# Linear attention of a decoder step: TensorE issues in the written order from the first head's gates on, small products gathered, output products one main product behind the state's

## The chip, the cores and the metric

The kernel runs on one core of one Trainium2 chip. Its time is the device time of one execution in microseconds (us), from the first to the last instruction and what lies around them. The five engines are named as in the profile: PE (TensorE matmuls; PEld are its weight loads), DVE (VectorE), ACT (ScalarE), POOL (GpSimd) and SP (SyncE, which issues most DMAs). Each engine works through its own queue in a fixed order, and semaphores make it wait for the others.

## The reference

One inference step of a two-layer decoder, for 512 new prompt positions and 8 decode positions, width 1024. Layer 0 mixes by windowed attention, layer 1 by gated linear attention (GLA); each is followed by a gated convolutional FFN, and each of the four parts ends in a LayerNorm. The change lies in the GLA, of which the reference computes, for each of 4 heads and in chunks of 64 positions:

```python
b = jnp.cumsum(lc, axis=2)                  # lc: log decay, from a product of rank 16
q_in = qc * jnp.exp(b)
k_in = kc * jnp.exp(-b)
att = jnp.where(causal, jnp.einsum('bhtd,bhsd->bhts', q_in, k_in), 0.0)
o = jnp.einsum('bhts,bhsv->bhtv', att, vc) + jnp.einsum('bhtd,bhdv->bhtv', q_in, S)
S_new = jnp.exp(b_last[:, :, 0, :, None]) * S + jnp.einsum('bhsd,bhsv->bhdv', kc * jnp.exp(b_last - b), vc)
...
o = o * lax.rsqrt(jnp.mean(jnp.square(o), -1, keepdims=True) + NORM_EPS) * norm_g
o = (o * jax.nn.silu(g)).reshape(B, T, GLA_DV)
return o @ w_o, s_new
```

## The kernel before

All activations lie transposed (channels on partitions). The positions are cut into two groups: `a`, the first 256 prompt positions, and `b`, the other 256 with the 8 decode positions. The weights come in units of 128 output channels. `plan` lists the units: for the GLA a rank-16 product for the decay (`gla_rank`), and per head one unit for q, one for k, two for v and two for the gate g; then 8 units of the output projection. `order` lets group b follow group a at a distance of 4 or 5 units. One unit of one group is a *main product*: `product` issues 24 matmuls (8 contraction blocks, times three terms of a high and low split in fp32r; L173 to L175) into one of 4 accumulator banks `accp`. The FFN's are the same or in a wider form (L191, L192).

Between main products lie the *small products* in plain fp32: the decay's (L681), the masked scores of a head (`att`, L730), the transposes of k and v (L750 to L752), the state's update `up` (L767), the two terms of the output `o` (L775 from the old state, L778 from the scores), the transposes of the normalised output for the gate (L866, L868), and those of the decode positions (L814 to L816, L827, L828). They use four more PSUM banks: `tp` (one), `pv` (one), `sc` (two).

The code is written as generators: `yield n` lets n main products pass ("slots") before the rest of a step is emitted; `due` resumes what has come due behind each main product. That sets the order in which the program is *written*. A list scheduler then orders each engine's queue by its own estimate of times, so the queue of PE may differ from the written order, and small products can come to stand inside a main product. `manual_schedule` over an engine keeps the written order on that engine. The weights of unit u+6 are loaded (SP, L156), rounded (ACT, L158) and reduced to their low part `wl` (DVE, L161) while unit u runs.

`ln_end` ends a LayerNorm: sums on PE (L256), the reciprocal root `r` on ACT and DVE (L267 to L277), subtraction of the mean on POOL and DVE (L263), then per channel block a product with r (`u`, L296), scaling on ACT (L297, the high part `xh` or `xs`) and POOL (L298), and the low part on DVE (L301, `xl` or `xs`). The main products of the next part wait for these.

Of the kernel before, what the change touches and what calls it, by code (L numbers as in the profile page):

```python
# [11 lines left out]
F32 = mybir.dt.float32  # L12
F32R = mybir.dt.float32r
I32 = mybir.dt.int32
AF = mybir.ActivationFunctionType
# [5 lines left out]
P = 128  # L21
# [70 lines left out]
class Net:  # L92
# [624 lines left out]
    def gla_k(self, g, u, h):  # L717
        nc, n = self.nc, g.n
        ps = self.product(g, u, g.xh, g.xl)
        yield 1  # L720
        g.k = self.gp.tile([P, n], F32, name=f"k_{g.name}")
        nc.vector.tensor_tensor(g.k, ps, g.em, op=ALU.mult)
        if g.i:
            g.kraw = self.gp.tile([P, NS], F32, name="kraw", bufs=2)
            nc.vector.tensor_copy(g.kraw, ps[:, 256:])
        yield 1
        att = self.mtile("sc")
        for b in range(2):
            bs = slice(b * P, (b + 1) * P)
            nc.tensor.matmul(att[:, bs], g.k[:, bs], g.q[:, bs], start=True, stop=True)  # L730
        g.att = self.attm[self.attm_i % 2]
        self.attm_i += 1
        nc.vector.copy_predicated(g.att, self.causal.unsqueeze(1).broadcast_to([P, 2, P]), att[:, :256].rearrange("p (b t) -> p b t", b=2))

    def gla_v(self, g, u, h, i):
        nc, n = self.nc, g.n
        ps = self.product(g, u, g.xh, g.xl)
        vt = self.gp.tile([P, n], F32, name=f"v{i}_{g.name}")
        nc.scalar.copy(vt, ps)
        if i == 0:  # L740
            g.v0 = vt
            return
        yield 1
        q, k, v0, v1, att, eb = g.q, g.k, g.v0, vt, g.att, g.eb
        ctx = dict(q=q, k=k, v0=v0, v1=v1, ep=g.ep, kraw=g.kraw) if g.i else None
        vks = []
        for b in range(2):
            bs = slice(b * P, (b + 1) * P)
            mp = self.mtile("tp")
            nc.tensor.transpose(mp[:, 0:P], k[:, bs], self.ident)  # L750
            nc.tensor.transpose(mp[:, P:2 * P], v0[:, bs], self.ident)
            nc.tensor.transpose(mp[:, 2 * P:3 * P], v1[:, bs], self.ident)  # L752
            vk = self.gp.tile([P, 3 * P], F32, name="vk", bufs=2)
            nc.scalar.copy(vk, mp[:, :3 * P])
            vks.append(vk)
        if g.i:
            self.spawn(self.gla_sample(g, h, **ctx), 0)
        yield 1
        o = self.mtile("pv")
        small = self.gp.tile([P, 8], F32, name="gsmall", bufs=2)  # L760
        st = self.tst[:, h]
        for b in range(2):
            bs = slice(b * P, (b + 1) * P)
            ob = o[:, b * 256:(b + 1) * 256]
            first = g.i == 0 and b == 0
            up = self.mtile("sc")[:, :256]
            nc.tensor.matmul(up, vks[b][:, 0:P], vks[b][:, P:], start=True, stop=True)  # L767
            if first:
                nc.vector.tensor_copy(st, up)
            else:  # L770
                f = self.gp.tile([P, 1], F32, name="f", bufs=2)
                nc.vector.tensor_tensor(f, self.ebl[:, h:h + 1], eb[:, 2 * b:2 * b + 1], op=ALU.mult)
                sp = self.gp.tile([P, 256], F32, name="sp", bufs=2)
                nc.vector.tensor_scalar(sp, st, f, None, op0=ALU.mult)
                nc.tensor.matmul(ob, q[:, bs], sp, start=True, stop=False)  # L775
                nc.vector.tensor_tensor(st, up, sp, op=ALU.add)
            nc.vector.tensor_copy(self.ebl[:, h:h + 1], eb[:, 2 * b + 1:2 * b + 2])
            nc.tensor.matmul(ob, att[:, b], vks[b][:, P:], start=first, stop=True)  # L778
        if g.i:
            so = self.gp.tile([P, 256], F32, name="sp", bufs=2)  # L780
            nc.vector.tensor_scalar(so, st, self.ebl[:, h:h + 1], None, op0=ALU.mult)
            nc.scalar.dma_start(out=self.O["gla_p"][h], in_=so)
        on = self.gp.tile([P, 512], F32, name="on", bufs=2)
        for b in range(2):
            ob = o[:, b * 256:(b + 1) * 256]
            nc.scalar.activation(on[:, b * 256:(b + 1) * 256], ob, AF.Square, accum_out=small[:, b:b + 1])
        rs = self.rms(small[:, 0:8], P, 2)
        for b in range(2):
            bs = slice(b * 256, (b + 1) * 256)
            nc.scalar.activation(on[:, bs], o[:, bs], AF.Copy, scale=rs[:, b:b + 1])  # L790
        g.on = on
# [13 lines left out]
    def gla_sample(self, g, h, q, k, v0, v1, ep, kraw):  # L805


        nc, st, g.st = self.nc, g.st, []
        nc.vector.tensor_copy(self.qz.rearrange("p (t x) -> p t x", t=2)[:, :, 0:P:32],
                              q[:, 256:].rearrange("p (t j) -> p t j", t=2))  # L810
        pr = self.gp.tile([P, NS], F32, name="qk")
        nc.vector.tensor_tensor(pr, q[:, 256:], k[:, 256:], op=ALU.mult)
        mp = self.mtile("tp")
        nc.tensor.transpose(mp[:NS, 0:P], v0[:, 256:], self.ident)  # L814
        nc.tensor.transpose(mp[:NS, P:2 * P], v1[:, 256:], self.ident)
        nc.tensor.matmul(mp[:NS, 256:257], pr, self.eps[:, 1:2], start=True, stop=True)  # L816
        vs = self.vs
        nc.vector.tensor_copy(vs[:NS], mp[:NS, :257])
        dv = self.dram.tile([NS, 256], F32, name="dv")
        nc.sync.dma_start(out=dv, in_=vs[:NS, :256])  # L820
        nc.vector.tensor_scalar(self.qkd[:NS].rearrange("p (j s) -> p s j", j=4)[:, 0:2],
                                self.ident[:NS, :NS].rearrange("p (t j) -> p t j", t=2), vs[:NS, 256:257], None, op0=ALU.mult)
        yield 1
        os_ = self.mtile("sc")[:, :256]
        for b in range(NS):
            r = slice(32 * (b % 4), 32 * (b % 4) + 32)
            nc.tensor.matmul(os_[r], self.qz[:, 32 * b:32 * b + 32], st[b // 2][:, b % 2], start=b < 4, stop=False)  # L827
        nc.tensor.matmul(os_, self.qkd, vs[:, :256], start=False, stop=True)  # L828
        small = self.gp.tile([P, 4], F32, name="ssmall")
        jk = self.gp.tile([P, 256], F32, name="sp", bufs=2)  # L830
        nc.scalar.activation(jk, os_, AF.Square, accum_out=small[:, 0:1])
        rs = self.rms(small, P, 1)
        g.os = self.gp.tile([P, 256], F32, name="osamp")
        nc.scalar.activation(g.os, os_, AF.Copy, scale=rs)
        yield SPAUSE if h < GH - 1 else SPAUSEL
        late = self.tc.keep_in_program_order
        for p in range(4):
            s = st[p]
            vb = self.gp.tile([P, 2, 256], F32, name="vb")
            nc.sync.dma_start(out=vb, in_=dv[2 * p:2 * p + 2].unsqueeze(0).broadcast_to([P, 2, 256]))  # L840
            yield 1
            for j in range(2):
                b = 2 * p + j
                late(nc.scalar.activation(s[:, j], s[:, j], AF.Copy, scale=ep[:, 256 + b:257 + b]))
                late(nc.vector.scalar_tensor_tensor(s[:, j], vb[:, j], kraw[:, b:b + 1], s[:, j], op0=ALU.mult, op1=ALU.add))  # L845
            nc.sync.dma_start(out=self.O["gla_s"][2 * p:2 * p + 2, h].rearrange("b k v -> k b v"), in_=s)
            if h < GH - 1:
                g.st.append(self.state_load(h + 1, p))
        if h == GH - 1:
            self.close(self.gp_cm)  # L850

    def gla_g(self, g, u, h, i):
        nc, n = self.nc, g.n
# [6 lines left out]
        nc.vector.reciprocal(e, e)  # L860
        sg = self.gp.tile([P, NT - 256], F32, name="sg", bufs=3)[:, :n]
        nc.vector.tensor_tensor(sg, ps, e, op=ALU.mult)
        yield 3 - i
        tp = self.mtile("tp")
        for b in range(2):
            nc.tensor.transpose(tp[:, b * P:(b + 1) * P], g.on[:, b * 256 + i * P:b * 256 + (i + 1) * P], self.ident)  # L866
        if g.i:
# [92 lines left out]
    def run(self):  # L960
        nc = self.nc
        self.plan()
        self.nu, self.extra, self.close_wx = WSLOTS, {}, False
        self.attn_open()
        self.later, self.slot, self.seq, self.pool_mark = [], 0, 0, None
        for i, u in self.order():
            g = self.groups[i]
            _, _, f, a, pre = self.units[u]
            if i == 0 and pre:
# [134 lines left out]
```

## Time and profile before

| | |
|---|---|
| median of 3 runs | 1148.62 us (1147.16 to 1149.75) |
| the profiled execution | 1146.73 us, of which the span of the instructions is 1144.7 us |
| mean granted clock of PE | 0.992 of full speed |
| busy share of the span | PE 96%, PEld 92%, DVE 69%, ACT 50%, POOL 29% |
| the GLA in the trace | its first product (rank, group a) at 528.6 us, the output projection done and the next LayerNorm under way at about 766 us |

Rows of the trace are read so. In a timeline: start in us from the span's start, length in us, engine, line, operation, out<-in, shapes, number of merged instructions, and in brackets how long the engine stood idle before it and who released it. An fp32 matmul shows as two or four instructions. Since matmuls are pipelined, the distance between starts is what one costs PE, not its length. In a view by stretches: the stretch, its length, then per engine the busy time and the number of instructions, the granted clock of PE (1.00 is full speed), the DMA share and GB/s. In a view of waits: who waited for whom, us in total, how many times, the longest.

### The profile page before, as it was taken

To read this page: it belongs to the slowest core of one execution; us is meant where nothing else is said; L and a number is where in the kernel's file an instruction comes from. 1 tells how busy PE (TensorE), PEld (TensorE's weight loads), DVE (VectorE), ACT (ScalarE), POOL (GpSimd) and SP (SyncE) were. 2 spreads that over 40 slices of the span, in tenths; PEclk is the share of its full clock that TensorE was granted. 3 is DMA by queue.
4 is the path that set the end of the run, shared out by engine and by line. 5 is a ranking of instruction groups with operands and counts; after the bars stand their busy time and mean duration, and the time that the engine had idled before them with its cause. 6 is when DMAs were issued, how large, how long until landed. Compare 5 with 4: busy or idle time off the path is not lost.

```text
span 1144.7 us, 22953 instructions
## 1 busy us (share of the span) xinstructions
PE 1104.2 (96%) x8806; PEld 1055.2 (92%) x8806; DVE 794.5 (69%) x1663; ACT 575.6 (50%) x1253; POOL 326.4 (29%) x556
## 2 busy tenths in 40 slices
PE   8999899999999999999899999989999999999995
PEld 8997798999999999998899999888999999999994
DVE  7897589655665566668867777799655665566657
ACT  5677457534553245435545556456524553245433
POOL 4575568100110011357300101287100110011344
PEclk9999999999999999999899999999999999999998
DMA  7553031323323233243124355341333232232222
GB/s 241 149 183 90 13 111 56 111 93 123 99 93 111 92 99 105 74 133 110 38 89 147 117 177 162 133 145 62 105 96 127 93 106 98 92 111 93 74 63 75
DMA packets 53789, 122.82 MB, mean 107 GB/s; under 512 B 6792, under 2 KB 27312, under 8 KB 53680
## 3 DMA queue, kind: packets, MB, share of 16 engines
q1 hardware_dynamic: 51664, 119.61, 32.4%
q10 hardware_dynamic: 2016, 1.75, 0.5%
q8 instruction: 69, 1.13, 0.4%
q14 instruction: 40, 0.33, 0.1%
HBM read 108.67 MB, written 8.47 MB: 102 GB/s over the span
## 4 chain that ended last, share of the span: by engine, by line
PE 70%; DVE 12%; DMA 6%; ACT 4%; POOL 4%; issue 4%; SPq 0%; ACTq 0%; DVEq 0%; POOLq 0%
PE accp L191 15%; PE accp L174 14%; PE accp L173 14%; PE accp L175 14%; PE accp L192 8%; DMA vb<-dv 3%; DVE wl L161 2%; POOL x_b L298 1%; DVE sgla L845 1%; DMA qs<-hl 1%; ACT wh L158 1%; POOL x_a L298 1%; DVE u L296 1%; PE pv L494 1%; DVE msq L276 1%
## 5 line engine op out<-in xcount | busy, mean ns | idle before, releaser
L161 DVE TENSOR_TENSOR wl<-raw,wh 128x1024 fp32r<-128x1024 f32 (+2 forms) x189 | 231.4, 1226 | 106.7 <-ACT wh L158 105.2
L158 ACT ACTIVATE wh<-raw 128x1024 fp32r<-128x1024 f32 (+2 forms) x185 | 191.9, 1037 | 215.0 <-PE accp L174 196.8
L173 PE MATMUL accp<-xh_b,wh 128*128 128x264 f32 x976 | 271.7, 279 | 2.5 <-DVE hprod L600 2.5
L174 PE MATMUL accp<-xl_b,wh 128*128 128x264 f32 x976 | 271.3, 278 | 0.2
L175 PE MATMUL accp<-xh_b,wl 128*128 128x264 f32 x976 | 270.8, 278 | 0.0
L191 PE MATMUL accp<-xs_a,wh 128*128 128x512 f32 x576 | 196.3, 382 | 0.0
L173 PEld LDWEIGHTS accp<-xh_b,wh 128*128 128x128 f32 x976 | 185.0, 190 | 3.5 <-DVE hprod L600 2.9
L174 PEld LDWEIGHTS accp<-xl_b,wh 128*128 128x128 f32 x976 | 184.9, 189 | 3.1 <-DVE xl_b L301 0.6
L175 PEld LDWEIGHTS accp<-xh_b,wl 128*128 128x128 f32 x976 | 184.8, 189 | 0.8 <-issue 0.6
L192 PE MATMUL accp<-xs_a,wl 128*128 128x256 f32 x576 | 145.4, 273 | 0.0
L173 PE MATMUL accp<-hh_b,wh 128*128 128x264 f32 x480 | 133.7, 279 | 3.3 <-ACT hh_b L198 3.3
L174 PE MATMUL accp<-hl_b,wh 128*128 128x264 f32 x480 | 134.3, 280 | 0.0
L175 PE MATMUL accp<-hh_b,wl 128*128 128x264 f32 x480 | 133.3, 278 | 0.0
L191 PEld LDWEIGHTS accp<-xs_a,wh 128*128 128x128 f32 x576 | 109.1, 189 | 11.4
L173 PE MATMUL accp<-xs_a,wh 128*128 128x256 f32 x400 | 112.3, 287 | 5.6 <-DVE x_b L219 2.1
L174 PE MATMUL accp<-xs_a,wh 128*128 128x256 f32 x400 | 112.4, 283 | 3.2 <-DVE xs_a L301 2.9
L192 PEld LDWEIGHTS accp<-xs_a,wl 128*128 128x128 f32 x576 | 110.2, 191 | 1.9
L175 PE MATMUL accp<-xs_a,wl 128*128 128x256 f32 x400 | 111.0, 280 | 0.7 <-DVE wl L161 0.5
L173 PEld LDWEIGHTS accp<-hh_b,wh 128*128 128x128 f32 x480 | 91.3, 190 | 3.8 <-ACT hh_b L198 3.6
L174 PEld LDWEIGHTS accp<-hl_b,wh 128*128 128x128 f32 x480 | 91.3, 190 | 1.4 <-issue 0.3
L175 PEld LDWEIGHTS accp<-hh_b,wl 128*128 128x128 f32 x480 | 91.3, 190 | 0.2
L202 POOL COPY hist<-aext 128x2 f32<-128x2 f32 x44 | 8.9, 203 | 284.4 <-DVE aext L578 281.3
(320 smaller groups left out, 2495.3 us busy)
## 6 DMA issues: line engine op xcount, KB each, us to landing
raw<-in_w_up SPq DMA_DIRECT2D x88, 512.0 KB, 3.4
raw<-in_w_down SPq DMA_DIRECT2D x32, 512.0 KB, 3.4
raw<-in_w_gla SPq DMA_DIRECT2D x24, 512.0 KB, 3.4
raw<-in_w_mix_o SPq DMA_DIRECT2D x16, 512.0 KB, 4.1
raw<-in_w_down SPq DMA_DIRECT2D x16, 384.0 KB, 3.1
qs<-hl SPq DMA_DIRECT2D x64, 64.0 KB, 2.1
sgla<-in_state_gla SPq DMA_DIRECT2D x16, 256.0 KB, 2.8
vb<-dv SPq DMA_DIRECT2D x16, 256.0 KB, 3.7
```

What stands on the lines that cost most here:

```text
L158: nc.scalar.activation(h[:, c], r[:, c], AF.Copy)
L161: nc.vector.tensor_tensor(l[:, c], r[:, c], h[:, c].bitcast(F32), op=ALU.subtract)
L173: nc.tensor.matmul(o, h[:, ks], xh, start=k == 0, stop=False)
L174: nc.tensor.matmul(o, h[:, ks], xl, start=False, stop=False)
L175: nc.tensor.matmul(o, l[:, ks], xh, start=False, stop=k == nt - 1)
L191: both = lambda: nc.tensor.matmul(o, h[:, ks], in_turn(rs[:, k].rearrange("p t q j -> p t (q j)")), start=k == 0, stop=last)
L192: low = lambda: nc.tensor.matmul(o[:, :P], l[:, ks], in_turn(rh[:, k]), start=False, stop=False)
L276: nc.vector.scalar_tensor_tensor(q, q, 0.5, nv, op0=ALU.mult, op1=ALU.mult)
L296: nc.vector.tensor_tensor(u, x[:, m], r, op=ALU.mult)
L298: ts = nc.gpsimd.tensor_scalar(x[:, m], u, sc(m), bi(m), op0=ALU.mult, op1=ALU.add)
L494: mm = nc.tensor.matmul(pv[64 * v:64 * v + 64, b * P:(b + 1) * P], self.vtok[:, kb, 64 * v:64 * v + 64], parts[v][w][:, b], start=i == 0, ...
L845: late(nc.vector.scalar_tensor_tensor(s[:, j], vb[:, j], kraw[:, b:b + 1], s[:, j], op0=ALU.mult, op1=ALU.add))
```

## The change

Seven edits, all in the GLA.

1. From the first head's gate product of group a until the first unit of the output projection, PE's queue keeps the written order.
2. The scores `att` go to the bank `pv` instead of `sc`.
3. The transposes of the second block of k and v go to `sc`, those of the first stay in `tp`, so that all six stand together. The gate's transposes likewise: first half `tp`, second half `sc`.
4. The state's two updates come first; the four products of the output come behind one more `yield 1`, the scores' term ahead of the state's.
5. The decode step (`gla_sample`) starts one slot later.
6. The decode output is copied out of its bank first (L838 of the changed kernel), and squared and scaled from the copy.
7. The two halves of a gate resume after 4 and 2 slots instead of 3 and 2, and so together.

```diff
@@ gla_k
-        att = self.mtile("sc")
+        att = self.mtile("pv")
@@ gla_v
-            mp = self.mtile("tp")
+            mp = self.mtile("sc" if b else "tp")
...
-            self.spawn(self.gla_sample(g, h, **ctx), 0)
+            self.spawn(self.gla_sample(g, h, **ctx), 1)
         yield 1
-        o = self.mtile("pv")
...
+        sps = []
         for b in range(2):
...
-                nc.tensor.matmul(ob, q[:, bs], sp, start=True, stop=False)
                 nc.vector.tensor_tensor(st, up, sp, op=ALU.add)
+            sps.append(sp)
...
-            nc.tensor.matmul(ob, att[:, b], vks[b][:, P:], start=first, stop=True)
+        yield 1
+        o = self.mtile("pv")
+        for b, sp in enumerate(sps):
+            ob = o[:, b * 256:(b + 1) * 256]
+            nc.tensor.matmul(ob, att[:, b], vks[b][:, P:], start=True, stop=sp is None)
+            if sp is not None:
+                nc.tensor.matmul(ob, q[:, b * P:(b + 1) * P], sp, start=False, stop=True)
@@ gla_sample
-        nc.scalar.activation(jk, os_, AF.Square, accum_out=small[:, 0:1])
+        g.os = self.gp.tile([P, 256], F32, name="osamp")
+        nc.scalar.copy(g.os, os_)
+        nc.scalar.activation(jk, g.os, AF.Square, accum_out=small[:, 0:1])
         rs = self.rms(small, P, 1)
-        nc.scalar.activation(g.os, os_, AF.Copy, scale=rs)
+        nc.scalar.activation(g.os, g.os, AF.Copy, scale=rs)
@@ gla_g
-        yield 3 - i
-        tp = self.mtile("tp")
+        yield 4 - 2 * i
+        tp = self.mtile("sc" if i else "tp")
@@ run
+        region = ExitStack()
         for i, u in self.order():
+            if (i, u) == (0, self.phases[3] + 5):
+                region.enter_context(self.tc.manual_schedule(engines={mybir.EngineType.PE}))
+            elif (i, u) == (0, self.phases[4]):
+                region.close()
```

The queues that come out of it, at the places of which the prediction speaks. Lines of the changed kernel are up to 7 higher (L766 is L767 of before, L782 is L778, L784 is L775, L833 is L827, L873 is L866).

PE, head 0, around the rank product of group b (L671, L672; the end of 16 matmuls is shown). Before: the scores come behind it, then the decay of head 1 (L681) and the first three transposes.

```order
L671 MATMUL accp<-xh_b,wh 128x264
L672 MATMUL accp<-xl_b,wh 128x264
L730 MATMUL sc<-q_a,k_a 128x128 x2
L681 MATMUL sc<-z_a,wa_6998 128x256
L750 MATMUL tp<-ident,k_a 128x128
L751 MATMUL tp<-ident,v_a 128x128
L752 MATMUL tp<-ident,v_a 128x128
L173 MATMUL accp<-xs_a,wh 128x256
```

After: the scores and all six transposes stand ahead of it; L681 stands 24 main matmuls earlier, ahead of the gate product whose last matmul is the first row.

```order
L175 MATMUL accp<-xs_a,wl 128x256
L730 MATMUL pv<-q_a,k_a 128x128 x2
L750 MATMUL tp<-ident,k_a 128x128
L751 MATMUL tp<-ident,v_a 128x128
L752 MATMUL tp<-ident,v_a 128x128
L750 MATMUL sc<-ident,k_a 128x128
L751 MATMUL sc<-ident,v_a 128x128
L752 MATMUL sc<-ident,v_a 128x128
L671 MATMUL accp<-xh_b,wh 128x264
L672 MATMUL accp<-xl_b,wh 128x264
```

So the rank product of b has moved behind everything that needs q and k of a.

ACT at the same time, before: the two exponentials of head 0's decay (`ep`, `em`, which q and k of a need) follow the last scaling of the LayerNorm.

```order
L692 ACTIVATE eb<-dcum 128x4
L297 ACTIVATE xh_b<-u,par 128x264
L698 ACTIVATE ep<-dcum 128x256
L699 ACTIVATE em<-dcum 128x256
L674 COPY z_b<-accp 128x264
```

After: the first two steps of head 1's decay stand ahead of them.

```order
L692 ACTIVATE eb<-dcum 128x4
L297 ACTIVATE xh_b<-u,par 128x264
L686 ACTIVATE de<-sc,par 128x256
L687 ACTIVATE de<-de 128x256
L698 ACTIVATE ep<-dcum 128x256
L699 ACTIVATE em<-dcum 128x256
```

DVE has one row more there too: L685 of head 1 stands ahead of the L696 of head 0.

PE, head 1, decode and output products of group b. Before: the decode's eight state products (L827) are split in two, with the second block's output products between them, all inside a main product.

```order
L173 MATMUL accp<-xh_b,wh 128x264
L827 MATMUL sc<-sgla,qz 32x256 x4
L775 MATMUL pv<-sp,q_b 128x256
L778 MATMUL pv<-vk,attm_6987 128x256
L827 MATMUL sc<-sgla,qz 32x256 x4
L174 MATMUL accp<-xl_b,wh 128x264
L828 MATMUL sc<-vsamp,qkd 128x256
```

After: one block, between two main products, with all four output products behind it.

```order
L175 MATMUL accp<-xs_a,wl 128x256
L833 MATMUL sc<-sgla,qz 32x256 x8
L834 MATMUL sc<-vsamp,qkd 128x256
L782 MATMUL pv<-vk,attm_6987 128x256
L784 MATMUL pv<-sp,q_b 128x256
L782 MATMUL pv<-vk,attm_6987 128x256
L784 MATMUL pv<-sp,q_b 128x256
L173 MATMUL accp<-xh_b,wh 128x264
```

The last head's is split in before too (1 and 7), and no longer.

DVE, in the LayerNorm of group a behind the output projection, before: a sum for group b (L249) stands ahead of the last step of r.

```order
L161 TENSOR_TENSOR wl<-raw,wh 128x1024
L249 TENSOR_TENSOR s_b<-s_b,sq 128x264
L277 SCALAR_TENSOR_TENSOR r<-msq,r 128x256
L263 TENSOR_TENSOR x_a<-x_a,mu 128x256 x2
L219 SCALAR_TENSOR_TENSOR x_b<-x_b,accp 128x264
```

After: it stands behind it.

```order
L161 TENSOR_TENSOR wl<-raw,wh 128x1024
L277 SCALAR_TENSOR_TENSOR r<-msq,r 128x256
L263 TENSOR_TENSOR x_a<-x_a,mu 128x256 x2
L249 TENSOR_TENSOR s_b<-s_b,sq 128x264
L219 SCALAR_TENSOR_TENSOR x_b<-x_b,accp 128x264
```

On POOL, in the same LayerNorm, the five subtractions of the mean (L263) stand ahead of the five products for the convolution's base (L558 to L562) instead of behind them. From there to the end the queues of before and after agree, and so they do up to head 0's gate product. On SP some weight loads of the GLA and of the output projection are issued one to five places later.

More of the change, by code (lines that the diff above doesn't have):

```diff
@@ L756, in gla_v @@
         if g.i:
-            self.spawn(self.gla_sample(g, h, **ctx), 0)
+            self.spawn(self.gla_sample(g, h, **ctx), 1)
         yield 1
-        o = self.mtile("pv")
         small = self.gp.tile([P, 8], F32, name="gsmall", bufs=2)
         st = self.tst[:, h]
+        sps = []
         for b in range(2):
-            bs = slice(b * P, (b + 1) * P)
-            ob = o[:, b * 256:(b + 1) * 256]
             first = g.i == 0 and b == 0
@@ L767, in gla_v @@
             nc.tensor.matmul(up, vks[b][:, 0:P], vks[b][:, P:], start=True, stop=True)
+            sp = None
             if first:
@@ L830, in gla_sample @@
         jk = self.gp.tile([P, 256], F32, name="sp", bufs=2)
-        nc.scalar.activation(jk, os_, AF.Square, accum_out=small[:, 0:1])
+        g.os = self.gp.tile([P, 256], F32, name="osamp")
+        nc.scalar.copy(g.os, os_)
+        nc.scalar.activation(jk, g.os, AF.Square, accum_out=small[:, 0:1])
         rs = self.rms(small, P, 1)
-        g.os = self.gp.tile([P, 256], F32, name="osamp")
-        nc.scalar.activation(g.os, os_, AF.Copy, scale=rs)
+        nc.scalar.activation(g.os, g.os, AF.Copy, scale=rs)
         yield SPAUSE if h < GH - 1 else SPAUSEL
```

## The prediction

> **What bounds the kernel now.** I read the page's busy times first, then the stretches around the change, then the waits of PE in them, then the timelines of the places that wait.
>
> ```profile
> PE 1104.2 (96%) x8806; PEld 1055.2 (92%) x8806; DVE 794.5 (69%) x1663; ACT 575.6 (50%) x1253; POOL 326.4 (29%) x556
> ```
>
> PE is the bound. The change removes no matmul and adds none, so it can only move time in which PE waits, runs at a lower clock, or pays for a change of shape. The stretches (busy us per engine, then PE's granted clock):
>
> ```profile
> 136.70:140.11 3.41, 3.41 (x23) 3.08 (x20) 1.26 (x3) 0.78 (x2) 0.14 (x2) 0.50 0.22 55
> ...
> 549.71:553.13 3.42, 1.88 (x12) 1.49 (x13) 3.12 (x8) 2.12 (x4) 3.25 (x3) 1.00 0.01 2
> 553.13:556.54 3.41, 2.82 (x8) 1.91 (x9) 2.59 (x11) 2.31 (x5) 0.92 (x2) 0.50 0.00 0
> 556.54:559.95 3.41, 3.41 (x16) 3.12 (x15) 1.95 (x3) 1.69 (x4) 0.00 (x0) 0.50 0.13 28
> ...
> 560.00:745.00 185.00, 183.03 (x1532) 173.70 (x1531) 138.57 (x330) 97.28 (x252) 20.00 (x27) 1.00 0.41 134
> 766.00:791.00 25.00, 19.99 (x163) 18.71 (x162) 24.53 (x50) 17.34 (x32) 21.96 (x22) 1.00 0.29 100
> ```
>
> From 560 to 745 us, nearly the whole GLA, PE idles 185.00 - 183.03 = 2.0 us. That is all that a better order can win there by waits. The dear places are at both ends: before 560, where the clock is halved, and after 766, where DVE is 98% busy and PE idles 5.0 us. The waits of PE from 560 to 745:
>
> ```profile
> PE tp L750 <- DVE sg L870: 0.8, 2, 0.6
> PE accp L173 <- ACT hh_b L198: 0.6, 1, 0.6
> PE tp L866 <- ACT on L790: 0.4, 1, 0.4
> PE sc L827 <- DVE tst L776: 0.2, 1, 0.2
> ```
>
> and the longest from 766 to 791:
>
> ```profile
> PE accp L174 <- DVE xs_a L301: 1.5, 1, 1.5
> PE accp L173 <- DVE hprod L600: 1.3, 1, 1.3
> PE accp L173 <- DVE x_b L219: 1.1, 1, 1.1
> PE accp L173 <- ACT xs_a L297: 0.8, 1, 0.8
> ```
>
> **Gathering itself.** What does a small product inside a main product cost?
>
> ```profile
> 597.38 0.28 PE L173 MATMUL accp<-xh_b,wh 128*128 128x264 f32 x1
> 597.50 0.59 PE L828 MATMUL sc<-vsamp,qkd 128*128 128x256 f32 x2
> 597.74 0.46 PE L174 MATMUL accp<-xl_b,wh 128*128 128x264 f32 x1
> 598.04 0.28 PE L175 MATMUL accp<-xh_b,wl 128*128 128x264 f32 x1
> ```
>
> From start to start a main matmul costs 0.11 us. From the lone L828 at 597.50 to the second main matmul at 598.04 are 0.54 us: 0.11 for one main, 0.43 for L828, two instructions of 0.21 to 0.22. Nothing is left for the switch, so gathering small products of the full width wins 0. It wins only where the decode's products are split, since these use a quarter of the array's columns each:
>
> ```profile
> 639.84 0.28 PE L173 MATMUL accp<-xh_b,wh 128*128 128x264 f32 x1
> 640.04 0.64 PE L827 MATMUL sc<-sgla,qz 128*32 128x256 f32 x8
> ...
> 642.24 0.38 PE L174 MATMUL accp<-xl_b,wh 128*128 128x264 f32 x1
> 642.46 0.59 PE L828 MATMUL sc<-vsamp,qkd 128*128 128x256 f32 x2
> ```
>
> Entering costs 0.20 instead of 0.11, and the matmul behind the block 0.22 instead of 0.11 (642.24 to 642.46): 0.2 to 0.3 us a block. Before there are 6 blocks in 4 heads, after 4. **Term 1: -0.5 us** (ends -0.6 and 0).
>
> **The start.** Around the rank product of group b, PE (first the decay product of head 0, then its gate product ending; L671 and L672 are the rank product):
>
> ```profile
> 542.62 0.66 PE L681 MATMUL sc<-z_a,wa 128*128 128x256 f32 x2
> ...
> 548.36 0.28 PE L175 MATMUL accp<-xs_a,wl 128*128 128x256 f32 x1
> 549.76 0.38 PE L671 MATMUL accp<-xh_b,wh 128*128 128x264 f32 x1 [1.13 <-ACT v_a L739]
> ...
> 554.95 0.59 PE L672 MATMUL accp<-xl_b,wh 128*128 128x264 f32 x1
> 555.77 1.22 PE L730 MATMUL sc<-q_a,k_a 128*128 128x128 f32 x4 [0.23 <-DVE k_a L722]
> 556.79 1.06 PE L681 MATMUL sc<-z_a,wa 128*128 128x256 f32 x2
> ```
>
> PE is through with the gate at 548.5 and waits for k of a until 555.77. Before, the 16 rank matmuls lie in this pause and cost the end nothing. After, the scores L730 stand ahead of them in a queue that keeps its order, so they come out of cover: 16 x 0.11 = 1.8 us of work at full clock. Into the pause moves instead only L681 of head 1 (0.43, as L828). The three transposes more that stand ahead of the rank product are moved, not added.
>
> When does k of a come? ACT and DVE:
>
> ```profile
> 553.55 0.62 ACT L297 ACTIVATE xh_b<-u,par 128x264 fp32r<-128x264 f32 x1 [0.69 <-DVE u L296]
> 554.51 0.42 ACT L698 ACTIVATE ep<-dcum 128x256 f32<-128x256 f32 x1 [0.34 <-DVE dcum L696]
> ...
> 553.92 0.56 DVE L696 TENSOR_SCALAR dcum<-dcum,bl 128x64 f32<-128x64 f32 x2
> 554.96 0.42 DVE L715 SCALAR_TENSOR_TENSOR q_a<-accp,ep 128x256 f32<-128x256 f32 x1
> 555.30 0.41 DVE L722 TENSOR_TENSOR k_a<-accp,em 128x256 f32<-128x256 f32 x1
> ...
> 567.89 0.48 DVE L685 TENSOR_SCALAR dmn<-sc,par 128x264 f32<-128x264 f32 x1
> ```
>
> After, DVE has L685 ahead of L696 (about 0.4: 553.92 becomes 554.3, its end 554.9), and ACT has L686 and L687 between L297 and L698: from 554.17, two rows of the length of L698 (0.42) in a chain, to about 555.0. So L698 starts about 0.4 to 0.5 later, and q, k and L730 with it: 556.2. Then the clock: it is at half from 553.13 to 559.95, two windows of 3.41. Work that starts at 556.2 runs at half speed for 3.8 us and loses 1.9; before it was 555.77 to 559.95, a loss of 2.1. **Term 2: 1.8 + 0.4 - 0.43 - 0.2 = +1.6 us.** Low end +1.2 (k not later); high end +3.3 (one more window at half clock, 3.41 / 2 = 1.7).
>
> Why the clock: 549.71 to 553.13 had PE 55% busy, and full clock was taken away at its end; 136.70 to 140.11, fully busy at half clock, was enough to get it back. [...]
>
> **The waits of the middle.** The four rows from 560 to 745 sum to 2.0. L750 waited for the single bank `tp`, of which a gate half was still being read; after, the gate halves stand two main products or more (5.4 us) ahead. The gate's transposes L866 stand three main products (8 us) behind the output. L827 stands a whole main product (2.7 us) behind the state's update. The output projection waited for `hh_b`; after, b's last gate transposes stand together, 38 main matmuls (4.2 us) ahead of its first product for b. All four causes go: **term 3: -2.0 us** (ends -2.0 and -1.0).
>
> **New waits.** A queue in written order stops wherever the row ahead is not ready, and everything behind it stands too. The tightest I find is b's first decay:
>
> ```profile
> 576.26 0.43 DVE L722 TENSOR_TENSOR k_b<-accp,em 128x264 f32<-128x264 f32 x1
> ...
> 578.61 0.61 PE L730 MATMUL sc<-q_b,k_b 128*128 128x128 f32 x4
> ```
>
> Before, k of b was ready 2 us ahead of its scores. After, PE reaches them about 577.5 (at full clock from 559.95: nine rank matmuls 1.0, two state products 0.9, the second gate 2.7, L681 0.4, three output products 1.3, four main products 10.7, four transposes some 0.4), and the chain to k shares one buffer (`de`) and ACT's and DVE's queues with the two gates of a; I follow it to about 577.8. Elsewhere a main product of 2.7 us lies between producer and user, and DVE is 138.57 / 185 = 75% busy. ACT's four copies more (0.4 each) lie in its 47% idle time; the state products in a row need both `sc` banks, freed a main product earlier. The weight loads that move on SP are six units ahead of use, and no wait above is for a weight: 0. **Term 4: +0.8 us** (ends 0 and +3.2, the largest row of this stretch, 0.8, in each of four heads); I take one such wait, since only one place is without slack.
>
> **The LayerNorm behind.**
>
> ```profile
> 764.01 0.96 DVE L249 TENSOR_TENSOR s_b<-s_b,sq 128x264 f32<-128x264 f32 x1
> 764.89 0.41 DVE L277 SCALAR_TENSOR_TENSOR r<-msq,r 128x256 f32<-128x256 f32 x1
> ```
>
> r of group a comes up to 0.88 earlier, but DVE has the same work in 766 to 791, and PE waits again for b and for DVE's `hprod`. **Term 5: -0.4 us** (ends -0.9 and 0).
>
> **Sum.** -0.5 + 1.6 - 2.0 + 0.8 - 0.4 = -0.5 us. The profiled execution took 1146.73 us (span 1144.7), so 1146.2 for one like it; it is 1.9 below the median of the runs, 1148.62, on which I put the difference: 1148.1. What a measurement can tell from no change is about 0.2%, 2.3 us, so this is no change.
>
> **Rivals.**
> - *Slower: the queue stops at b's first scores.* If the chain to k of b takes 3 us longer than I follow it (for a at head 0, from L681 at 542.62 to L722, it took 12.7 us beside the LayerNorm), L730 of b waits 3.3 instead of 0.3, the four banks `accp` stay full and PE has nothing else. Sum +2.5, 1151.1. It decides from a wait there of 3 us on. Against it: no LayerNorm competes then. Chance 0.14.
> - *The clock falls otherwise.* The pause of PE after is 548.9 to 556.2 without a break, 7.3 us, before it held the rank product. If the windows lie so that work after the pause runs at half speed for two windows (6.8 us), or before's pause does not cost the clock, +1.5 to +2.1: sum about +1.3, 1149.9. Both halvings in the trace lie on one grid of 3.41, which speaks for a free grid; that 55% busy was not enough speaks against before escaping. [...] Chance 0.10, a third of it beyond +2.3.
> - *Faster: the LayerNorm pays.* POOL subtracts the mean ahead of the convolution's base, r comes 0.9 earlier, and the 5.0 us of waits after 766 halve; with no new wait: -0.5 + 1.6 - 2.0 - 2.5 = -3.4, 1145.2. It needs DVE's slow rows (0.96 instead of 0.41 while POOL works) to fall where nobody waits. Chance 0.27.
> - *The forecast*, -2.3 to +2.3: 0.49.
>
> **Range and chances.** With the rivals inside to nearly their full prices, 1145.2 to 1151.1 leaves out about 2 in 10. The likeliest case's own range is 1146.3 to 1150.9. Faster 0.27; slower 0.14 + 0.03 = 0.17; within 0.2%: 0.49 + 0.07 = 0.56.
>
> **What would show it.** In the trace after: L730 of a starts at 556.2 with the rank product of b right behind the transposes and a pause of 7 us ahead (term 2); half clock over 553 to 560; one block of decode products per head (term 1); no wait between 565 and 745 above 0.5 us but at L730 of b (terms 3 and 4); r of a 0.9 earlier relative to the last product of the output projection (term 5). Wrong would be: a chain to k that is shorter, so that the rank product is not late; waits of over 1 us each head; or waits after 766 that fall by more than 1 us.

## The result, and the profile after

The changed kernel takes 1168.21 us, median of 5 runs (1167.35 to 1170.71), the kernel before 1148.57 beside it (1147.16 to 1149.75): ratio 1.0175, 95% interval 1.0159 to 1.0192, 19.6 us slower. The forecast was no change, 1148.1 (1145.2 to 1151.1). The profiled execution's span is 1166.3 us, against 1144.7 before; these lie 21.6 apart, since the profiled execution of before is 1.8 below its median.

The page's busy times after; PE has the same 8806 matmuls:

```profile
PE 1107.8 (95%) x8806; PEld 1059.7 (91%) x8806; DVE 795.1 (68%) x1663; ACT 577.9 (50%) x1257; POOL 319.1 (27%) x556
```

The stretches after, in the columns of those before (busy us per engine, PE's granted clock, DMA share, GB/s). The first three are the windows of the pause at the start, the fourth is the rest of the linear attention, the next two are a pair of neighbouring clock windows (the stretches of 3.41 us on whose edges the granted clock changes), the last is the LayerNorm behind:

```profile
550.30:553.72 3.42, 0.02 (x1) 0.00 (x0) 3.11 (x8) 2.52 (x6) 2.97 (x4) 0.99 0.01 2
553.72:557.13 3.41, 0.00 (x0) 0.00 (x0) 3.38 (x14) 2.51 (x8) 1.41 (x2) 0.50 0.00 0
557.13:560.55 3.42, 3.07 (x14) 3.07 (x15) 3.35 (x8) 1.95 (x7) 0.41 (x1) 0.51 0.00 0
560.55:766.00 205.45, 193.95 (x1588) 184.66 (x1586) 138.52 (x326) 99.73 (x252) 22.97 (x32) 0.98 0.38 121
621.86:625.27 3.41, 0.69 (x6) 0.47 (x5) 1.75 (x7) 0.84 (x2) 0.00 (x0) 1.00 0.93 279
625.27:628.69 3.42, 3.42 (x18) 3.42 (x17) 2.12 (x6) 1.63 (x4) 0.00 (x0) 0.51 0.47 147
787.30:812.30 25.00, 19.18 (x156) 17.96 (x155) 24.55 (x51) 17.02 (x31) 22.27 (x23) 1.00 0.28 96
```

PE idles 205.45 - 193.95 = 11.5 us where it idled 2.0 before. And in that stretch and just behind it four windows (from 625.27, 673.05, 727.69 and 768.69) run at half clock, each behind a window in which PE was less than half busy (0.69, 1.23, 1.41 and 1.45 of 3.41 us; the first pair is shown); PE is busy in them for 3.42, 2.87, 2.69 and 3.41 us. In the first of them main matmuls start 0.22 us apart (625.52 to 628.38), behind it 0.11 (from 628.79); so half of that busy time, 6.2 us, is an estimate of what the half clock costs. PE's waits after, from 560 to 770:

```profile
PE tp L873 <- ACT on L796: 5.4, 2, 2.7
PE tp L752 <- ACT v_b L739: 2.7, 1, 2.7
PE accp L175 <- DVE wl L161: 2.5, 3, 1.1
PE accp L173 <- ACT wh L158: 1.7, 2, 1.2
PE sc L766 <- DVE tst L769: 1.0, 2, 0.5
```

L873 (the gates' transposes) and L752 (a transpose of v) have taken the place of the small waits of before. Three of the four waits that were counted as a gain are gone, 1.6 of 2.0 us (no row for L750, for `hh_b` or for the decode's L833 is left); the fourth, the gates' transposes, has grown from 0.4 to 5.4, and PE's idle time as a whole is six times as large. The statistics of a's next LayerNorm, L256, start at 776.9, before at 755.6: 21.3 later, 1.3 of it there when the layer begins (L681 of head 0 at 543.88, before 542.62). Behind, nothing comes back.

**Why PE stands at L873.** The chain from the output to the normalised output at the first of two such stops (621.9 and 670.9), rows of PE, ACT and DVE after in the order of the chain:

```profile
613.24 0.59 PE L784 MATMUL pv<-sp,q_a 128*128 128x256 f32 x2
615.27 1.21 DVE L161 TENSOR_TENSOR wl<-raw,wh 128x1024 fp32r<-128x1024 f32 x1
616.87 0.16 DVE L803 TENSOR_SCALAR gsmall<-gsmall 128x2 f32<-128x2 f32 x1
618.56 1.74 DVE L867 RECIPROCAL de<-de 128x256 f32<-128x256 f32 x1
620.22 0.09 DVE L806 TENSOR_TENSOR gsmall<-gsmall 128x2 f32<-128x2 f32 x1
622.11 0.14 DVE L807 SCALAR_TENSOR_TENSOR gsmall<-gsmall 128x2 f32<-128x2 f32 x1
622.73 0.88 DVE L852 SCALAR_TENSOR_TENSOR sgla<-vb,kraw,sgla 128x256 f32<-128x256 f32 x2 [0.40 <-DMA vb<-dv]
623.86 0.15 DVE L808 SCALAR_TENSOR_TENSOR gsmall<-gsmall 128x2 f32<-128x2 f32 x1
624.04 0.84 ACT L796 ACTIVATE on<-pv,gsmall 128x256 f32<-128x256 f32 x2 [3.05 <-DVE gsmall L808]
624.57 0.69 PE L873 MATMUL tp<-ident,on 128*128 128x128 f32 x2 [2.68 <-ACT on L796]
```

The steps on `gsmall` are 0.1 to 0.2 us each, but each stands in DVE's queue behind a reciprocal, a weight's conversion or the decode's state update. The output ends at 613.8, `on` at 624.9: 11 us. The text leaves three main products, 8 us. Before, the same chain was nearly as long, and PE did not wait for it here (0.4 us at the second place, 670.0):

```profile
611.50 0.59 PE L778 MATMUL pv<-vk,attm 128*128 128x256 f32 x2
619.93 0.15 DVE L800 TENSOR_TENSOR gsmall<-gsmall 128x2 f32<-128x2 f32 x1
621.53 0.16 DVE L802 SCALAR_TENSOR_TENSOR gsmall<-gsmall 128x2 f32<-128x2 f32 x1
621.73 0.84 ACT L790 ACTIVATE on<-pv,gsmall 128x256 f32<-128x256 f32 x2 [1.44 <-DVE gsmall L802]
624.13 0.27 PE L866 MATMUL tp<-ident,on 128*128 128x128 f32 x1
```

From 612.1 to 622.6 are 10.5 us; the free order had put main products ahead of L866, which started 1.6 us after `on` was there.

### The profile page after: what moved, and what is told of

The parts are those of the page before. It is cut to its first block, busy times and chain, and to the rows that moved or that the text cites. A ratio compares the mean times of both kernels' runs of the same rounds, so it can differ in the third digit from the quotient of the medians.

```text
span 1166.3 us, 22968 instructions
## 1 busy us (share of the span) xinstructions
PE 1107.8 (95%) x8806; PEld 1059.7 (91%) x8806; DVE 795.1 (68%) x1663; ACT 577.9 (50%) x1257; POOL 319.1 (27%) x556
## 4 chain that ended last, share of the span: by engine, by line
PE 72%; DVE 10%; POOL 4%; issue 4%; DMA 4%; ACT 3%; SPq 0%; ACTq 0%; DVEq 0%; POOLq 0%
PE accp L191 15%; PE accp L174 15%; PE accp L175 15%; PE accp L173 15%; PE accp L192 7%; DVE wl L161 2%; DMA vb<-dv 2%; POOL x_b L298 1%; DMA qs<-hl 1%; POOL x_a L232 1%; ACT wh L158 1%; POOL x_a L298 1%; DMA raw<-in_w_qkv 1%; DVE u L296 1%; DVE sgla L852 1%
```

## The experiments

All times are medians beside runs of the kernel before on the same chip (1148.6 to 1149.5). The theories: O, the kept order is the cost, not the edits; G, the chain to the gates' transposes; W, SP's queue and late weights; V, DVE standing for the decode's `vb`; S, weights' slots held until b's use.

**Edits alone** (`e1_edits_alone`: the region removed, all else as after).

```diff
-            if (i, u) == (0, self.phases[3] + 5):
-                region.enter_context(self.tc.manual_schedule(engines={mybir.EngineType.PE}))
-            elif (i, u) == (0, self.phases[4]):
-                region.close()
```

> The six edits of the program's text without the written order of TensorE. If the order is what costs (theory O), the scheduler again puts each small product where its operands are ready: 1148.6 within 3 us, no wait of PE above 1 us between 565 and 745. If the edits themselves cost (rival: later outputs, later decode), about half of the 20 us stays, 1155 to 1165.

1152.66 us, ratio 1.0034 (1.0021 to 1.0047): 3.7 over before, a little outside theory O's 3, and with one wait of 2.1 us (for a state's transfer, at the decode's L833) that it had excluded. By far the larger part of the 19.6 us is the order, not the edits.

**Order alone** (`e2_order_alone`: the same four lines put into before, with none of the edits).

> The kernel of before with TensorE in program order over the same stretch and none of the six edits. Theory O (a kept order pays for every wait whose price the program's text doesn't cover): slower than after, 1170 to 1185, since the outputs stand directly behind the state's products and the gates' transposes 2 to 3 slots behind. Rival (the edits are the cost): near 1150.

1173.31, ratio 1.0207 (1.0192 to 1.0223), as O had it: the kept order costs 24.4 without the edits. The edits do what they were written for (the waits for the single bank `tp`, L750, are 10.2 us here and none after), and not enough of it.

**Gates' transposes later** (`e3_gate_later`).

```diff
-        yield 4 - 2 * i
+        yield 4 - 2 * i + (2 if h < GH - 1 else 0)
```

> After, with the gates' transposes of the first three heads two main products (5.4 us) later. Theory G (the chain from the output to its transposes takes 10.5 us where the text gives 8): both waits of 2.9 us at the gates' transposes (621.6 and 670.6) and the windows at half clock behind them (1.6 each) go, 9 us: 1159. Theory W (the queue of SP and the late weights carry the loss): these waits turn into others, at most 3 us less, 1165 to 1168.

1168.98, ratio 1.0176 (1.0158 to 1.0193): nothing won. G's 1159 is out, and W's range ends 1 below. The waits at L873 for `on` (5.4) are gone, and nearly as much has come at v_b, 7.5 instead of 2.7. PE's waits here, 560 to 757, and DVE's and ACT's rows ahead of the first of them:

```profile
PE tp L752 <- ACT v_b L739: 7.5, 3, 3.4
```

```profile
627.63 0.88 DVE L852 SCALAR_TENSOR_TENSOR sgla<-vb,kraw,sgla 128x256 f32<-128x256 f32 x2 [2.77 <-DMA vb<-dv]
634.02 0.88 DVE L852 SCALAR_TENSOR_TENSOR sgla<-vb,kraw,sgla 128x256 f32<-128x256 f32 x2 [3.32 <-DMA vb<-dv]
634.82 0.48 DVE L877 SCALAR_TENSOR_TENSOR sg<-sc,par,sg 128x256 f32<-128x256 f32 x1
```

```profile
635.33 0.43 ACT L198 ACTIVATE hs_a<-sg 128x256 fp32r<-128x256 f32 x1 [4.16 <-DVE sg L877]
635.67 1.04 ACT L158 ACTIVATE wh<-raw 128x1024 fp32r<-128x1024 f32 x1
636.61 0.36 ACT L739 COPY v_b<-accp 128x264 f32<-128x264 f32 x1
```

Three queues pass the wait on: DVE stands 3.32 us for the transfer `vb`, the gate's product stands behind it; ACT stands 4.16 us for that gate; the copy of v_b stands behind it on ACT, and PE behind the copy. That is a new theory, V.

**SP in program order too** (`e4_sp_in_order`).

```diff
-                region.enter_context(self.tc.manual_schedule(engines={mybir.EngineType.PE}))
+                region.enter_context(self.tc.manual_schedule(engines={mybir.EngineType.PE, mybir.EngineType.SP}))
```

> After, with SyncE's queue in program order too over the same stretch, so that the decode's transfers and the weights' loads alternate as written. Theory W: the weights are no longer late and ACT doesn't stand behind a missing weight (0.7, 1.2, 0.8, 2.9, 1.4, 0.9 us of waits, 1.6 for the half clock behind the 2.9): 9 us less, 1159. Theory G: the two waits at the gates' transposes stay as they are (2.9 each with 1.6 behind) and the time falls by 3 us at most.

1210.55, ratio 1.0533 (1.0517 to 1.055), 42 us worse than after, and neither theory's number. The order of SP's queue matters, then, but the written one is far worse; what SP's order in after costs, this run doesn't show. PE's waits from 540 to 830, then SP's rows of one stretch (SPq is the time of issuing):

```profile
PE accp L173 <- ACT wh L158: 34.8, 7, 9.4
```

```profile
599.80 0.33 SPq L156 DMA_DIRECT2D raw<-in_w_gla  x1
621.92 0.40 SPq L853 DMA_DIRECT2D out_gla_s<-sgla  x1
...
632.55 0.37 SPq L156 DMA_DIRECT2D raw<-in_w_gla  x1
```

Each pair of the decode's states goes out, is read in for the next head (into the same rows, so after it is out) and asks for the next `vb`, and SP stands at each; no weight is asked for between 599.80 and 632.55. With SP in the scheduler's order (after) the weights stand ahead of that block, three in one go, and the first state goes out after them:

```profile
596.54 20.30 SPq L156 DMA_DIRECT2D raw<-in_w_gla  x3
618.66 0.39 SPq L853 DMA_DIRECT2D out_gla_s<-sgla  x1
```


**v broadcast once a head** (`e5_vb_once`: three of four transfers `vb` gone, so the update of six of the eight tokens uses wrong values).

```diff
-            vb = self.gp.tile([P, 2, 256], F32, name="vb")
-            nc.sync.dma_start(out=vb, in_=dv[2 * p:2 * p + 2]...)
+            if p == 0:
+                vb = ...; nc.sync.dma_start(...)
```

> After, with v of the decode tokens broadcast once a head instead of once for each pair of them (so the state update of six of the eight tokens uses wrong values; the instructions of VectorE and ScalarE stay, three of four transfers vb go). Theory V (VectorE's kept order stands up to 4 us for each vb, and the gates, ScalarE's v copies and the weights' conversions stand behind it): VectorE's waits for vb fall from 12.8 us to under 4, the waits of TensorE at L873 and at v_b's transposes go, 9 to 13 us less: 1155 to 1159. Theory S (a slot of weights is held until group b has used it, four units after a, so a weight is converted only just ahead of its use and ScalarE stands in the conversion): the waits move, 4 us less at most: 1164 to 1168.

1164.49, ratio 1.0134 (1.0119 to 1.0148). 3.7 us less: in S's range, not V's 9 to 13. DVE no longer waits for `vb`, the wait at v_b is gone, but the one at the gates' transposes is still there, here 5.9 us:

```profile
PE tp L874 <- ACT on L796: 5.9, 2, 3.0
```

**b three units behind a** (`e6_lag3`).

```diff
-                lead = max(LAG, min(top, p0 + 2 * top - u))
+                lead = 3 if p0 == self.phases[3] else max(LAG, min(top, p0 + 2 * top - u))
```

> After, with group b three units behind a in this layer instead of four to five, so a weight's slot is free a unit (5.4 us) earlier. Theory S: ScalarE's waits in the conversion (28.9 us for TensorE) fall by more than half, TensorE's waits for weights (0.7, 1.2, 0.8, 1.4, 0.9) and for v_b (2.9) go, with the half clock behind them 9 to 11 us less: 1157 to 1159. Theory V: VectorE's waits for vb stay at about 13 us and with them the two waits at the gates' transposes; 3 us less at most, 1165 to 1168.

1163.8, ratio 1.0128 (1.0111 to 1.0144), 4.4 us less than after, between the theories. S's premise was not met: ACT's waits in the conversion fall to 23.5 from 28.9, not by half. The waits at L873 and at v_b are gone, but b's scores now wait 6.4 us for a bank that the same chain frees (and behind 757 one weight still 2.7):

```profile
PE pv L730 <- ACT on L796: 6.4, 4, 2.0
```

A third place, and the same chain.

**Without the decode's state update** (`e7_after_no_update` on after, `e8_before_no_update` on before: `vb`, L851 and L852 left out, so the states go out unchanged; all other transfers stay).

```diff
-            vb = ...; nc.sync.dma_start(out=vb, ...)
...
-                late(nc.scalar.activation(s[:, j], s[:, j], AF.Copy, scale=...))
-                late(nc.vector.scalar_tensor_tensor(s[:, j], vb[:, j], kraw[:, b:b + 1], s[:, j], ...))
```

> After without the decode's state update (its output is the old state): no vb, no L851 and L852; the transfers of the state in and out stay. If the loss is the kept order meeting the decode's update (V): 14 us less than after, 1152 to 1156, and within 5 us of the same cut made in before. If the kept order costs by itself: 5 us less at most, and 15 us or more above the same cut in before.

> Before without the decode's state update (its output is the old state): the control for the run above. Before's waits in the middle sum to 2 us, so 1144 to 1149 under every theory.

After: 1148.87, ratio 0.9992 (0.9983 to 1.0002). Before: 1144.06, ratio 0.9956 (0.9944 to 0.9969). The cut is worth 19.3 us in after (more than V's 14) and 5.0 in before: the kept order meeting the decode's update is 14.3 of the 19.6 us. 4.8 us stay between the two.

The rows of `on`, here and in `e5_vb_once`, tell the chain to the gates' transposes from the wait for `vb`:

```profile
620.29 0.84 ACT L796 ACTIVATE on<-pv,gsmall 128x256 f32<-128x256 f32 x2 [0.43 <-DVE gsmall L808]
```

```profile
624.12 0.84 ACT L796 ACTIVATE on<-pv,gsmall 128x256 f32<-128x256 f32 x2 [3.33 <-DVE gsmall L808]
```

Without the update the output ends at 613.5 and `on` at 621.1, 7.6 us, within the 8 that the text leaves. With the update, but without a wait for `vb`, it takes 11.3 (613.6 to 625.0), as long as in after. So the update's own rows in the queues of ACT and DVE make this chain too long, not the transfer `vb`; what went with the wait for `vb` is the stop at v_b.

For the 4.8 us that stay, PE's waits in after without the update, 540 to 757; there is none at the gates' transposes or at L752:

```profile
PE pv L730 <- DVE k_a L722: 7.2, 1, 7.2
PE accp L175 <- DVE wl L161: 1.1, 1, 1.1
PE sc L766 <- DVE tst L769: 1.0, 2, 0.5
PE accp L173 <- ACT wh L158: 0.6, 1, 0.6
```

**Both mends together** (`e9_gate_later_vb_once`: the edits of `e3_gate_later` and `e5_vb_once`).

> After with both the gates' transposes two main products later and v broadcast once a head (as in the two runs before, so the same wrong values in six of eight states). If the two causes stand for each other (whichever is taken away, TensorE stops at the other), now both are gone: 1150 to 1156, no wait of TensorE above 1.3 us but the pause. If it is the update's own work on VectorE and ScalarE (8 x 0.44 and 8 x 0.45 us a head) that makes the chain long: the waits stay, 1159 or more.

1155.4, ratio 1.0054 (1.0037 to 1.0072): 12.8 us less than after, where the one alone gave -0.8 and the other 3.7. Both causes together, as the first of the two readings had it. In 560 to 757 no row of waits above 1.4 us is left, and the mean granted clock is 0.992, as in before (after: 0.985). Whichever of the two was mended alone, PE stopped at the other.

**The start** (`e10_no_update_late_region`: `e7_after_no_update` with the written order from the second head's gates on).

```diff
-            if (i, u) == (0, self.phases[3] + 5):
+            if (i, u) == (0, self.phases[3] + 11):
```

> The cut of the decode's state update in after, with the written order beginning at the second head's gates instead of the first's. Between this cut in after (1148.9) and in before (1144.1) are 4.8 us. If they come from the start (the pause of 7.3 us with the rank product behind it, and the two late weights behind that, 0.7 and 1.2 us): 1144 to 1146. If they come from the order of the later heads: 1148 to 1149.

1144.25, ratio 0.9954 (0.9941 to 0.9967): 4.6 us less than with the order from the first head on, so what stays lies in the first head, where the pause is. The two waits at L766 are still there and cost nothing that could be told.

**Two buffers vb** (`e11_before_two_vb` on before; `e12_mended` on after, with the gates' transposes and the later start of the order as above).

```diff
-            vb = self.gp.tile([P, 2, 256], F32, name="vb")
+            vb = self.gp.tile([P, 2, 256], F32, name="vb", bufs=2)
...
-            sb = c("sb")
+            sb = c("nv")
...
-                sa = c("sa")
+                sa = c("msq")
```

> Before with two buffers vb instead of one (room for it from two scratch rows of the LayerNorm that share a buffer with rows of its end). VectorE waits 15.4 us for vb before, but TensorE only 2 us in the middle: 1146 to 1149. The control for the next run.

> After with three mends: the gates' transposes two main products later, two buffers vb, the written order from the second head's gates on. If the causes found so far are all there is: 1144 to 1149, as fast as before or faster. If three weight loads in a row on SyncE ahead of the first state going out hold the chain as before: 1153 to 1160.

Before with two buffers: 1151.31, ratio 1.0021 (1.0009 to 1.0032), just slower, above its range. Its profiled execution has two waits that before doesn't have in this size (1.9 us for ACT's L198, 1.7 for L297, before 0.6 and 0.8) and a mean granted clock of 0.988, before 0.992; whether this comes from the second buffer or from the shared scratch rows isn't shown. The mended kernel: 1151.3, ratio 1.0019 (1.001 to 1.0027). It takes back 17 of the 19.6 us and is no faster than before. It lies between the two ranges: the causes found aren't quite all there is, and whether the three weights in a row on SP hold the rest isn't settled. What is left in 560 to 757 are its waits for v_b, the bank of L730 and one state:

```profile
PE tp L752 <- ACT v_b L739: 1.4, 1, 1.4
PE pv L730 <- ACT on L796: 1.1, 2, 0.6
PE sc L766 <- DVE tst L769: 1.0, 2, 0.5
PE sc L833 <- DMA sgla<-in_state_gla: 0.6, 1, 0.6
```

No run points to a version faster than before. How the 17 us divide between order, `vb` and start in the full kernel isn't told apart further, since the parts don't add.

## Why the prediction was wrong

- **Term 3 (-2.0, the waits of the middle go) failed at its step for the gates' transposes**: "stand three main products (8 us) behind the output". The distance was right; that it was enough was not read from the trace. The chain takes 10.5 us in the trace of before, rows of which were at hand, so the step should have read a stop of 2.5 us at such a place. Measured: 2.7 us at two places, 5.4 in all. Of the four causes of before three did go, 1.6 us; this fourth one, priced as a gain of 0.4, became the largest loss.
- **Term 4 (+0.8, ends 0 and +3.2) failed twice.** "Elsewhere a main product of 2.7 us lies between producer and user" counted distances on PE and not the queues in between; the high end came from waits of an order that moves out of the way, which says nothing of one that doesn't. And "the weight loads ... are six units ahead of use ...: 0": a slot of weights is held until b has used it, four to five units after a, so the conversion stands on ACT until PE lets go of the slot. ACT's longest rows, before and after, 560 to 760:

```profile
ACT wh L158 <- PE accp L174: 17.5, 11, 2.4
```

```profile
ACT wh L158 <- PE accp L174: 28.9, 17, 4.5
```

  That the real lead is short was visible before the change. The one place that was priced, b's first scores, has no wait after (L730 at 580.71).
- **No term held the clock behind a stop.** The prediction had halving only at the start. Each of four windows that held 2.0 to 2.7 us of waits was followed by one at half clock, together an estimated 6.2 us, more than half as much as the waits added from 560 on (9.5 to 766 and 2.0 behind).
- **Term 2 (+1.6, ends +1.2 and +3.3) had the right mechanism; what else the start costs was in no term.** L730 of a was to start at 556.2; it starts at 557.48 in a layer that begins 1.26 later, which is 556.2. The pause (7.2 us without a break), the rank product behind it and half clock over two windows came as told. The start by stretches, from the same product (L681) on, before and then after:

```profile
542.62:560.00 17.38, 14.17 (x86) 12.34 (x85) 14.16 (x34) 10.31 (x21) 9.14 (x11) 0.80 0.04 8
```

```profile
543.88:560.55 16.67, 9.51 (x68) 9.21 (x67) 15.68 (x39) 10.41 (x25) 9.38 (x12) 0.80 0.01 2
```

  PE idles 7.2 us instead of 3.2 and loses 1.5 to the half clock instead of 3.1 (half of 3.07, and of 2.82 and 3.41): 2.4 us. That is good to about 1 us, since a matmul that stands alone counts as busy for its whole length (0.28 us or more, against 0.11 from start to start in a row). The two late weights behind the pause, 0.6 and 1.1, were in no term. Measured, the first head costs 4.6 (`e7_after_no_update` less `e10_no_update_late_region`); the last half microsecond isn't resolved.
- **Term 1** can't be told from the rest: the blocks stand once a head as told, and 0.5 us is below what these runs resolve.
- **Term 5 (-0.4)**: r of a came 1.1 earlier against L256, a little more than the 0.9 counted (row below: 785.05 - 776.9 = 8.2, before 764.89 - 755.6 = 9.3), and bought nothing: in the same 25 us PE is busy 19.18 instead of 19.99.

```profile
785.05 0.71 DVE L277 SCALAR_TENSOR_TENSOR r<-msq,r 128x256 f32<-128x256 f32 x1
```

- **The rivals**: the slower one had the right sentence (a queue in written order stops at the row that isn't ready) at the wrong place, with a price that the whole range followed.

The sum with what was measured: 9.5 (waits in 560 to 766, 11.5 - 2.0), 6.2 for the four windows at half clock, 2.0 of waits for weights behind 766 (1.2 and 0.8), and 2.4 at the start make 20.1, against 20.0 (21.3 less 1.3) between the same two places.

## What to carry to other kernels

Before fixing an engine's order, measure in the old trace how long each chain between two of its rows really takes, queues of the other engines included, and compare that with the distance in the new order: a free order hides a chain of 10.5 us, a kept one shows what lies beyond 8. Two late chains can stand for each other, so a mend that wins nothing alone may be half of one; cutting out the suspected work in both kernels (19 us against 5) sized the cause where single mends could not. And count a lead in units from the time when the buffer comes free, not from the number of buffers.

## What the runs showed of the hardware

The clock behind a stop, in the traces of before and after. In before the window from 549.71, in which PE was busy for 1.88 of 3.42 us (55%), was followed by two at half clock. In after each of the four windows with the long waits (busy for 0.69, 1.23, 1.41 and 1.45 of 3.41 us, 20% to 43%) was followed by one. The busy time alone doesn't tell them apart: two windows of after with PE busy for 1.85 of 3.42 us (54%, from 785.82) and 1.90 of 3.41 (56%, from 789.24) were followed by full clock (1.00). The four held 2.0 to 2.7 us of waits each, and the half clock behind them came to 1.3 to 1.7 us more, as an estimate: half of the busy time there, 2.69 to 3.42 us. What decides between full and half clock isn't shown here.
